# Head 1's output gates and values by seven half-size products, with the low parts of the sums of x on VectorE

## The chip, the cores and the metric

The kernel runs on one core of one Trainium2 chip. The metric is the device time of one execution in microseconds (us); the kernel before takes 1049.19 us (median of 3 runs, 1048.17 to 1050.72).

## The reference

One inference step of a two-layer decoder trunk. 1024 prompt tokens and 8 sequences of 4 new tokens, 1056 tokens in all, pass a gated linear recurrence (layer 0) and then HGRN2 attention with 8 heads of 128 channels (layer 1), each with a normalisation ahead, a projection in and a projection out. The change lies in layer 1:

```python
xn = _rmsnorm(x, g_norm)                        # (tokens, 1024)
u = (xn @ w_in).astype(jnp.float32)             # (tokens, 4 * 1024)
q, f, iv, gate = jnp.split(u, 4, axis=-1)       # per head: 128 columns of each
q = silu(q); log_g = ...f...; k = 1 - exp(log_g)
# chunked linear attention of every head over q, k, v = iv, decay log_g, state S
y = o * rsqrt(mean(o * o) + EPS) * o_gain * silu(gate)
return x + y @ w_out
```

A head has four projections, called items here: 0 queries, 1 forget gates, 2 values, 3 output gates. Each is a product of xn (1056 x 1024) with 1024 x 128 weights. All is float32.

## The kernel before, in words

**Products in three parts.** Every float32 operand is kept as a high part (hi) and a low part (lo) in the type fp32r, and a product is three matmuls (`mm3`, L253): L255 w_hi·x_hi, L256 w_hi·x_lo, L257 w_lo·x_hi. xn lies in SBUF as `xh` and `xl`, 8 tiles of 128 channels by 1056 tokens. A high part is a cast on ScalarE (ACT); a low part is a subtraction, `subtract` (L339), on GpSimd (POOL) or VectorE (DVE), whichever is passed to it as `e`.

**Direct items.** `product` (L405) makes one item for a third of the tokens (a chunk of 352): 8 tiles times 3 matmuls of 128 x 352. Heads 0 and 1 (`HC = 2`) are made so, one item and chunk after the other.

**Items by seven products.** From head 2 on, `seven(h, a, b, order, at)` makes two items a and b of a head together, by Strassen's scheme: seven products p1 to p7, each 512 channels by half the tokens, instead of eight. Each is made for two quarters of the tokens (x = 0, 1; 264 columns) in 4 x 3 matmuls, so a call has 7 x 2 x 12 = 168 matmuls of 128 x 264, and VectorE adds the products up (`plus`, L1521, 14 a call). The weights are combined by VectorE (`combine`, L1458, 4 of 512 columns a call), cast on ScalarE (L1448) and their low parts subtracted on GpSimd in halves of 256 columns (L339, `wlo`). `order` is a string such as "126b74b35": digits are products in order, "b" is the place of a *burst*, that is a piece of the attention of a head (`burst1` to `burst4`: its scores, its states and its outputs at several levels).

**Sums of x.** The products read x itself (p1, p2, p3) or sums of its quarters. Three of these sums, T2, T3 and T4 (tiles `t20` to `t41`; in lists of instructions `t_5227` and `t_5228` are T2 hi and lo, `t_5229` and `t_5230` T3, `t_5231` and `t_5232` T4), serve p6, p7 and p4. They are built once, in `build` and `parted_sum`, while heads 0 and 1 are projected: for each of 4 tiles and 2 quarters four loads of xn (264 columns each) into landing spots, three sums or differences by VectorE (L1389), three casts by ScalarE (L1392) and three low parts on GpSimd (L339): 24 of each in all. The landing spots are a ring of six pieces: two of the small tile `tmp` and four in `R[:, 3]`. The fourth one, T1, serves p5 and is written over the upper halves of `xh[0..3]` and `xl[0..3]` once nothing direct reads them any more (`build1`): 8 pieces, each with two loads, a difference (L1389), a cast (L1392) and a low part on VectorE (L339), through the two pieces of `tmp` as a ring.

**What sets the order.** The kernel isn't written out instruction by instruction: a list planner (`Flow`) is given every instruction with a priority and a modelled cost and writes one order for each engine; the engines then run their queues in order. `SPOTS` names after which direct chunk of head 1 the bursts stand. DMAs are issued by SyncE (SP) for the most part, and each waits there until its target is free.

**Around the change**, before: after head 0 stand head 1's items 0, 1, 3 and 2 by 12 direct products, with burst 1 and burst 2 of head 1 among the last six; then head 2 with its items 0 and 1 by `seven` in the order `FQ0 = "126b74b35"`. For head 1's item 1 ScalarE makes a tanh (L1031) and GpSimd two scalings (L1033 into `ST`, L1035 into `a`); from `ST` VectorE makes the decays in `R` by one operation over all tokens (L1087), and the scores of burst 1 (L1075) start from those.

Of the kernel before, what the change touches and what calls it, by code (L numbers as in the profile page):

```python
# [26 lines left out]
NMM = 3  # L27
HC = 2
NM7 = 3
FQ0, FQ, GV = "126b74b35", "12b675b43", "126b754b3"  # L30
CUT = 2
SPOTS, SPOTS0, SPOTS1 = (6, 9, 0, 2), (2, 5, -1, -1), (1, 5, 9, 13, 17, 20)
K2 = 8 - K1
RM, SM = 3, 6
OUT = ((0, 512), (512, 288), (800, 256))
# [5 lines left out]
TOK = SEQ + NB * NS  # L41
# [5 lines left out]
H = 8  # L47
EPS = 1e-6
HT, QT = TOK // 2, TOK // 4
# [174 lines left out]
def tile_trunk(ctx: ExitStack, tc: tile.TileContext, xT, prm, hc, w0, wg, wo0, w1, wo1, s_in,  # L224
               yT, h_out, c_out, sp_out, ss_out):
    nc = tc.nc
    V, S, G, T, Q = nc.vector, nc.scalar, nc.gpsimd, nc.tensor, nc.sync
# [11 lines left out]
    R = work.tile([128, 4, TOK], F32, tag="R", name="R")  # L239
# [10 lines left out]
    def chunk(c):  # L250
        return slice(c * CH, (c + 1) * CH)
# [59 lines left out]
    with ExitStack() as l0:  # L311
# [3 lines left out]
        def fixed(name, shape, dt=F32, pool=None):  # L315
            return (pool or pl).tile(shape, dt, tag=name, name=name)
# [10 lines left out]
        def act(n, emit, r, w, prio=5, more=0.0):  # L327
            fl.add("ACT", (0.09 + 0.00088 * n if fl.exact else 0.25 + 0.0007 * n) + more, emit, r, w, prio)
# [615 lines left out]
    with ExitStack() as l1:  # L944
# [6 lines left out]
        TB = {(n, i): fixed(f"t{n}{i}", [128, 4, HT], F32R, p1) for n in (2, 3, 4) for i in range(2)}  # L951
        tmp = fixed("tmp", [128, 2, QT], F32, p1)
# [19 lines left out]
        SG = [rows[1 + 2 * (h % 2)] for h in range(H)]  # L972
# [6 lines left out]
        SA = a_rows[1]  # L979
# [8 lines left out]
        def two(*name):  # L988
            return [(*name, i) for i in range(2)]
# [4 lines left out]
        def brow(h, i):  # L994
            return (Bs, eight("B")) if i else (B2, eight("B2"))
# [7 lines left out]
        def inherit(new, olds):  # L1003

            fl.readers.setdefault(new, []).extend(i for k in olds for i in (*fl.readers.get(k, ()), *([fl.writer[k]] if k in fl.writer else [])))
# [3 lines left out]
        def ykeys(m, a, n):  # L1009

            return [("Y", m, i) for i, (u, v) in enumerate(zip(CUTS, CUTS[1:])) if u < a + n and v > a]

        def thrice(o, x, r, key):

            act(96, lambda: S.copy(o.rearrange("p (j t) -> p j t", j=3), x[:, None, :].to_broadcast([128, 3, 32])), r, ((key,),), 2)

        def item(h, i):


            def evac(c, ps, pk):  # L1020
                q = chunk(c)
                ps = ps[:, :CH]
                if i == 2:
                    n = min(CH, SEQ - c * CH)
                    act(n, lambda: S.copy(VT[:, c * CH:c * CH + n], ps[:, :n]), (pk,), (("VT", c),), 0)
                    if n < CH:
                        thrice(vrep, ps[:, n:], (pk,), "vrep")
                    return
                if i == 1:
                    t, tk = next(ts)  # L1030
                    act(CH, lambda: S.activation(t, ps, AF.Tanh, scale=0.5), (pk,), (tk,), 0)  # L1031
                    g, (b, bk) = Gs, brow(h, 1)
                    pool(0.3 * CH, lambda: G.tensor_scalar(g[:, q], t, lc[:, h:h + 1], lbc[:, h:h + 1], op0=ALU.mult, op1=ALU.add),  # L1033
                         (tk,), GK, 0)
                    pool(0.3 * CH, lambda: G.tensor_scalar(b[:, q], t, lcn[:, h:h + 1], lc[:, h:h + 1], op0=ALU.mult, op1=ALU.add),  # L1035
                         (tk,), bk, 0)
                else:
                    o, k = (SG[h], ykeys(h % 2, c * CH, CH)) if i else arow(h, 0)
                    act(CH, lambda: S.activation(o[:, q], ps, AF.Silu), (pk,), k, 0)

            return w1[4 * h + i], evac
# [42 lines left out]
        def own_gate(h):  # L1084
            decay[h] = Gs, *GK
            (a, k0), (a1, k1) = arow(h, 0), arow(h, 1)
            dve(TOK, lambda: V.tensor_tensor(a1, a, Gs, op=ALU.mult), (*k0, *GK), k1, 1, True)  # L1087
# [258 lines left out]
        def burst1(h):  # L1346
            s = next(hg)
            run(together([*([levels01(h, *s)] if h < H else []), *([keys_(h - 1, *s), values(h - 1, *s)] if h else [])]))

        def burst2(h):  # L1350
            s = next(hg)
            run(together([*([levels24(h, *s)] if h < H else []), *([states(h - 1, *s), advance(h - 1, 0)] if h else [])]))

        def burst3(h):
            s = next(hg)
            run(together([*([outs(h - 1, *s), advance(h - 1, 1)] if h else []), *([levels816(h, *s)] if h < H else [])]))

        def burst4(h):
            s = next(hg)
            run(together([*([gated(h - 1, *s)] if h else []), *([levels3264(h, *s)] if h < H else [])]))  # L1360
            k = ()
            if h < H:
                turned(h, "vt", VT, [("VT", c) for c in range(4)], vflat, VK, vflat, VK)
                keys_turned(h)
                k = (("kt", "d", h % 2),)
            if 0 < h < H:
                dma(si.rearrange("p b v -> p (b v)"), s_in[h], k, two("si"), 4, 512)
            if 0 < h < H - 1:
                dma(yd[h - 1], SG[h - 1], (*ykeys((h - 1) % 2, 0, TOK), ("kt", 1)), (("yd", h - 1),), 4, 528)


        def build(j, temps):

            for x in range(2):
                lo, up = slice(x * QT, x * QT + QT), slice(HT + x * QT, HT + x * QT + QT)
                got = []
                for m, q in ((j + 4, up), (j, up), (j, lo), (j + 4, lo)):
                    t, tk = next(temps)
                    dma(t, xnd[m][:, q], (), (tk,), 5, 132)
                    got.append((t, tk))  # L1380
                (t, tk), (u, uk), (l, lk), (d, dk) = got
                add(QT, t, t, u, ALU.subtract, (tk, uk), tk)
                add(QT, l, l, t, ALU.add, (tk, lk), lk)
                add(QT, d, d, l, ALU.subtract, (dk, lk), dk)
                for n, o, k in ((3, t, tk), (2, l, lk), (4, d, dk)):
                    parted_sum(n, j, x, TB[n, 0][:, j, lo], TB[n, 1][:, j, lo], o, k, G)

        def add(n, o, a, b, op, r, w, prio=5):
            dve(n, lambda: V.tensor_tensor(o, a, b, op=op), r, (w,), prio, True)  # L1389
# [1 line left out]
        def parted_sum(n, j, x, hi, lo, t, tk, e, prio=5):  # L1391
            act(QT, lambda: S.copy(hi, t), (tk,), (("T", n, 0, j, x),), prio)  # L1392
            subtract(e, QT, lo, t, hi, (tk, ("T", n, 0, j, x)), (("T", n, 1, j, x),), prio)
# [143 lines left out]

        dma(si.rearrange("p b v -> p (b v)"), s_in[0], (), two("si"), 4, 512)
        own_gate(0)
        spots = [(R[:, 3, i * QT:i * QT + QT], ("tmp", 2 + i)) for i in range(4)]  # L1540
        small_ = [(tmp[:, i], ("tmp", i)) for i in range(2)]
        temps = cycle(small_ + spots)
        for j in range(4):
            build(j, temps)
        for h in range(HC):
            order = [item(h, i) for i in ((0, 1, 3, 2) if h else (3, 2))]
            seq_ = [(i, c) for i in range(len(order)) for c in range(NCH)]
            if h == HC - 1:
                seq_ = seq_[:-6] + [(len(order) - 2 + i, c) for c in (2, 1, 0) for i in (0, 1)]
            ws2 = {} if h else ahead  # L1550
            for n, (i, c) in enumerate(seq_):
                if i not in ws2:
                    ws2[i] = weights(order[i][0], 1024)
                order[i][1](c, *product(ws2[i], xcols(c)))
                if h and n == 5:
                    own_gate(h)
                for j, b in enumerate((burst1, burst2, burst3, burst4)):
                    if n == (SPOTS0, SPOTS)[h][j]:
                        b(h if j < 2 else h - 1)
# [3 lines left out]
        for i in range(6):  # L1563
            key = ("s", i)
# [3 lines left out]
        rawq = [next(raws) for _ in range(NRAW)]  # L1568
        for i in range(5 - NRAW):
            key = ("W", i)  # L1570
            inherit(key, [k for _, k in spots])
            rawq.append((R[:, 3, i * HT:i * HT + 512], key))


        for h in range(HC, H):
            seven(h, 0, 1, FQ0 if h == HC else FQ, (lambda h=h: burst3(h - 1), lambda h=h: burst4(h - 1)))
            own_gate(h)
            seven(h, 3, 2, GV, (lambda h=h: burst1(h), lambda h=h: burst2(h)))


        yh, yl = (list(o[:4]) for o in (xh, xl))
# [4 lines left out]
        for k in range(H):  # L1586
            if k < 4:
                olds = [("x", 1, k, x) for x in range(2)] + [("T", 1, i, k, x) for i in range(2) for x in range(2)]
            else:
                n, i = ((2, 0), (3, 0), (4, 0), (4, 1))[k - 4]  # L1590
# [22 lines left out]
        for i, o in enumerate(ks):  # L1613
            key = ("k", i, 1)
# [18 lines left out]
        for n, (m, c) in enumerate([(m, c) for c in range(NCH) for m in range(2)] + [(m, c) for m in range(2, KD) for c in range(NCH)]):  # L1633
# [9 lines left out]
            x, xk = x2[m][:, chunk(c)], ykeys(Y2 + m, c * CH, CH)  # L1643
# [13 lines left out]
        for m in range(KD):  # L1657
            row = (xh, xl)[m // 4][4 + m % 4]
            hi, lo, hk, lk = row[:, :nl], row[:, nl:2 * nl], ("late", m, 0), ("late", m, 1)
# [9 lines left out]
        for o, olds in ((R[:, 0], eight("A", 1)), (SA, [("SA", i) for i in range(2)]), (rows[5], VK),  # L1669
                        (SG[6], ykeys(0, 0, TOK))):  # L1670
            for a in (0, 512):
                key = ("spare", len(spare))
# [50 lines left out]
        for a, n in OUT:  # L1723
# [4 lines left out]
            for m in range(KD):  # L1728
# [5 lines left out]
                hi, lo, wk = late[m]  # L1734
# [7 lines left out]
                x, xk = x2[m][:, q], ykeys(Y2 + m, a, n)  # L1742
# [89 lines left out]
```

## Time and profile before

The profiled execution took 1049.25 us, of which its span (first to last instruction) is 1047.4 us.

| what | before |
|---|---|
| time, median of 3 runs | 1049.19 us |
| the profiled execution: time, span | 1049.25, 1047.4 us |
| busy: PE (matmul), DVE (VectorE) | 99%, 77% |
| busy: ACT (ScalarE), POOL (GpSimd) | 55%, 50% |
| chain that ended last: PE, DVE | 89%, 7% |
| TensorE from head 1's item 1 to the end of its direct products | 550.0 to 591.15 us |

In the page, engines are PE (TensorE's matmuls), PEld (its weight loads), DVE, ACT, POOL and SP; L339 is line 339 of the kernel. A row of a group gives `output<-inputs`, the shape, the count, the busy time and mean duration, and the idle time ahead of it with its releaser. Where the matmuls fill TensorE, an instruction of another engine costs time only if a matmul comes to wait for it.

### The profile page before, as it was taken

What the parts mean: (1) busy time and instruction counts of PE and PEld (TensorE: products, weight loads), DVE (VectorE), ACT (ScalarE), POOL (GpSimd) and SP (SyncE); (2) the same over time, 40 slices, a digit from 0 to 9 for tenths busy, and PEclk for the clock granted to TensorE, in tenths of its full rate; (3) what the DMA queues carried; (4) which work ended last, traced back from release to release, by engine and by line L of the source; (5) the groups of instructions that cost most, each with busy time, mean ns of one, the idle gap of its engine ahead of it and who ended that gap; (6) DMA issues with size and microseconds to landing.
All of it is one profiled execution on the core that took longest, in us unless ns stands there. A gap on an engine that the chain in (4) does not pass through costs nothing.

```text
span 1047.4 us, 25549 instructions
## 1 busy us (share of the span) xinstructions
PE 1036.1 (99%) x9836; PEld 1006.4 (96%) x9836; DVE 805.7 (77%) x1578; ACT 579.9 (55%) x1324; POOL 524.1 (50%) x601
## 2 busy tenths in 40 slices
PE   9999999999999999999999999999999999999997
PEld 9999999999999999999999999999999999999986
DVE  7999996788788599345586787897979797985436
ACT  6568656866775776334444364646454554652333
POOL 3425443544544255644756555555555555651544
PEclk9999999999999999999999999999999999999998
DMA  9201112123761586434554341423324242577204
GB/s 303 65 16 58 54 49 73 49 65 94 218 194 58 160 270 187 151 123 169 185 153 149 95 157 61 121 87 114 114 92 130 78 143 85 182 225 210 86 1 166
DMA packets 92009, 130.66 MB, mean 125 GB/s; under 512 B 11632, under 2 KB 70000, under 8 KB 91888
## 3 DMA queue, kind: packets, MB, share of 16 engines
q1 hardware_dynamic: 82672, 113.69, 34.9%
q10 hardware_dynamic: 9216, 15.35, 4.7%
q8 instruction: 77, 1.26, 0.5%
q14 instruction: 44, 0.36, 0.1%
HBM read 85.93 MB, written 38.20 MB: 119 GB/s over the span
## 4 chain that ended last, share of the span: by engine, by line
PE 89%; DVE 7%; DMA 1%; issue 1%; POOL 1%; ACT 0%; POOLq 0%; ACTq 0%; DVEq 0%
PE mm L255 25%; PE mm L257 25%; PE mm L256 25%; PE hg L1075 1%; PE hg L583 1%; PE hg L1289 1%; PE hg L255 1%; PE hg L1291 1%; PE hg L256 1%; PE hg L257 1%; PE hg L1237 1%; DMA wraw<-in_w_dram 1%; DVE R L449 1%; PE mm L1075 1%; PE hg L1266 1%
## 5 line engine op out<-in xcount | busy, mean ns | idle before, releaser
L255 PE MATMUL mm<-xh,whi 128*128 128x352 f32 (+1 forms) x1143 | 358.9, 314 | 0.6 <-DVE k L1521 0.6
L257 PE MATMUL mm<-xh,wlo 128*128 128x352 f32 (+1 forms) x1143 | 353.3, 309 | 0.0
L256 PE MATMUL mm<-xl,whi 128*128 128x352 f32 (+1 forms) x1143 | 353.0, 309 | 0.0
L339 POOL TENSOR_TENSOR wlo<-wraw,whi 128x256 fp32r<-128x256 f32 (+3 forms) x184 | 200.3, 1104 | 197.9 <-ACT whi L394 94.8
L255 PEld LDWEIGHTS mm<-xh,whi 128*128 128x128 f32 x1143 | 214.7, 188 | 2.9 <-DVE k L1521 1.0
L256 PEld LDWEIGHTS mm<-xl,whi 128*128 128x128 f32 x1143 | 214.9, 188 | 1.5
L257 PEld LDWEIGHTS mm<-xh,wlo 128*128 128x128 f32 x1143 | 214.8, 188 | 0.3 <-POOL wlo L339 0.3
L515 DVE SCALAR_TENSOR_TENSOR k<-xb,prm_sb,k 128x352 f32<-128x352 f32 (+2 forms) x144 | 90.0, 637 | 10.9 <-ACT k L512 7.7
L255 PE MATMUL mm<-t,whi 128*128 128x264 f32 (+1 forms) x306 | 89.4, 292 | 0.0
L257 PE MATMUL mm<-t,wlo 128*128 128x264 f32 (+1 forms) x306 | 87.6, 286 | 0.0
L256 PE MATMUL mm<-t,whi 128*128 128x264 f32 (+1 forms) x306 | 87.5, 286 | 0.0
L339 POOL TENSOR_TENSOR wlo<-R,whi 128x256 fp32r<-128x256 f32 x64 | 59.0, 941 | 32.9 <-ACT whi L1448 14.7
L1521 DVE TENSOR_TENSOR k<-mm,k 128x264 f32<-128x264 f32 x144 | 59.9, 423 | 19.0 <-PE mm L257 18.3
L598 POOL TENSOR_TENSOR k<-X 128x352 f32<-128x352 f32 x36 | 45.8, 1282 | 48.4 <-DVE R L599 39.2
L394 ACT CAST whi<-wraw 128x512 fp32r<-128x512 f32 (+2 forms) x83 | 46.3, 574 | 37.4 <-PE mm L256 18.7
L255 PEld LDWEIGHTS mm<-t,whi 128*128 128x128 f32 x306 | 57.5, 188 | 0.5
L256 PEld LDWEIGHTS mm<-t,whi 128*128 128x128 f32 x306 | 57.6, 188 | 0.0
L257 PEld LDWEIGHTS mm<-t,wlo 128*128 128x128 f32 x306 | 57.6, 188 | 0.0
L1448 ACT CAST whi<-wraw 128x512 fp32r<-128x512 f32 x52 | 32.0, 617 | 33.6 <-PE mm L256 14.1
L255 PE MATMUL mm<-yh,whi 128*128 128x352 f32 x153 | 49.9, 326 | 0.0
L257 PE MATMUL mm<-yh,wlo 128*128 128x352 f32 x153 | 49.4, 323 | 0.0
L256 PE MATMUL mm<-yl,whi 128*128 128x352 f32 x153 | 49.4, 323 | 0.0
(457 smaller groups left out, 2537.6 us busy)
## 6 DMA issues: line engine op xcount, KB each, us to landing
wraw<-in_w_dram SPq DMA_DIRECT2D x57, 256.0 KB, 3.1
wraw<-in_w_dram ACTq DMA_DIRECT2D x35, 256.0 KB, 3.2
wraw<-in_wo_dram SPq DMA_DIRECT2D x34, 192.0 KB, 2.6
si<-in_s_in_dram SPq DMA_DIRECT2D x8, 512.0 KB, 5.8
vt<-sg SPq DMA_DIRECT2D x8, 512.0 KB, 3.2
sg<-vt SPq DMA_DIRECT2D x32, 128.0 KB, 2.9
kt<-kt SPq DMA_DIRECT2D x8, 512.0 KB, 2.6
sg<-kt SPq DMA_DIRECT2D x32, 128.0 KB, 3.4
```

The lines of the kernel that those rows point to most:

```text
L255: T.matmul(out, wh, xh, start=first, stop=False)
L256: T.matmul(out, wh, xl, start=False, stop=False)
L257: T.matmul(out, wl, xh, start=False, stop=last)
L339: emit = lambda: e.tensor_tensor(b, x, a.bitcast(F32), op=ALU.subtract)
L394: act(m, lambda hi=hi, raw=raw, m=m: S.copy(hi[:, :m], raw[:, :m]), rk, (hk,), prio)
L449: (pool if e is G else dve)(CH, lambda: e.tensor_tensor(a[:, :CH], a[:, :CH], sq, op=ALU.add), (sk, ak), (ak,), 2)
L515: dve(u, lambda src=src, dst=dst, sh=sh, k=k: V.scalar_tensor_tensor(dst, sh(src, k), pc("cw", 12 * k + m), dst, op0=ALU.mult, op1=ALU.add ...
L583: fl.add("PE", 0.62, lambda ps=ps, i=i, c=c: T.matmul(ps[:96, :CH], gs[:, i, :], ST[:96, chunk(c)], start=True, stop=True), (("gs",), *((" ...
L598: pool(CH, lambda x=x, a=a, b=b: G.tensor_tensor(x, a.bitcast(F32), b.bitcast(F32), op=ALU.add), (ak, bk), (xk,), 3)
L1075: T.matmul(ps[32 * j:32 * j + 32, n * w:n * w + w], B[:, o:o + 32], q(slice(o, o + 32)), start=True, stop=True, tile_position=(0, 32 * j))
L1448: act(512, lambda: S.copy(hi, raw), (rk,), (hk,), 2)
L1521: dve(QT, lambda: V.tensor_tensor(o[0], z[0], u[0], op=ALU.add), (z[1], u[1]), (o[1],), 0)
```

## The change

- Head 1 makes only its items 0 and 1 by direct products; its items 3 and 2 go through `seven(1, 3, 2, GV0)`, with `GV0 = "126b74b35"`, and bursts 1 and 2 of head 1 stand at the two "b" of it. Item 1's chunks run from the last to the first. Head 2's first call loses its own order and takes that of the later heads (`FQ = "12b675b43"`).
- The 24 low parts of T2, T3 and T4 are subtracted by VectorE (`V`), no longer by GpSimd (`G`).
- The pieces of xn for T2 to T4 land in eight spots in rows that are used later (`SG[1]`, head 1's output gates, in lists of instructions `sg`, and `SA`, in lists `a`), no longer in two of `tmp` and four of `R[:, 3]`; `R[:, 3]`, which holds raw weights in `seven`, no longer has to wait for them. The pieces are built first for quarter 0 of all four tiles, then for quarter 1.

```diff
-FQ0, FQ, GV = "126b74b35", "12b675b43", "126b754b3"
+FQ, GV0, GV = "12b675b43", "126b74b35", "126b754b3"
...
-SPOTS, SPOTS0, SPOTS1 = (6, 9, 0, 2), (2, 5, -1, -1), (1, 5, 9, 13, 17, 20)
+SPOTS, SPOTS0, SPOTS1 = (-1, -1, 0, 2), (2, 5, -1, -1), (1, 5, 9, 13, 17, 20)
...
-        def build(j, temps):
+        def build(x, temps):
 
-            for x in range(2):
+            for j in range(4):
...
                 for n, o, k in ((3, t, tk), (2, l, lk), (4, d, dk)):
-                    parted_sum(n, j, x, TB[n, 0][:, j, lo], TB[n, 1][:, j, lo], o, k, G)
+                    parted_sum(n, j, x, TB[n, 0][:, j, lo], TB[n, 1][:, j, lo], o, k, V)
...
-        spots = [(R[:, 3, i * QT:i * QT + QT], ("tmp", 2 + i)) for i in range(4)]
+        spots = [(o[:, i * QT:i * QT + QT], ("spot", n, i)) for n, o in enumerate((SG[1], SA)) for i in range(4)]
         small_ = [(tmp[:, i], ("tmp", i)) for i in range(2)]
-        temps = cycle(small_ + spots)
-        for j in range(4):
-            build(j, temps)
+        temps = cycle(spots)
+        for x in range(2):
+            build(x, temps)
+        for n, keys in enumerate((ykeys(1, 0, TOK), two("SA"))):
+            for k in keys:
+                inherit(k, [k for _, k in spots[4 * n:4 * n + 4]])
         for h in range(HC):
-            order = [item(h, i) for i in ((0, 1, 3, 2) if h else (3, 2))]
+            order = [item(h, i) for i in ((0, 1) if h else (3, 2))]
             seq_ = [(i, c) for i in range(len(order)) for c in range(NCH)]
             if h == HC - 1:
-                seq_ = seq_[:-6] + [(len(order) - 2 + i, c) for c in (2, 1, 0) for i in (0, 1)]
+                seq_ = seq_[:-6] + [(len(order) - 2 + i, c) for i in (0, 1) for c in (2, 1, 0)]
...
             key = ("W", i)
-            inherit(key, [k for _, k in spots])
             rawq.append((R[:, 3, i * HT:i * HT + 512], key))
 
-        for h in range(HC, H):
-            seven(h, 0, 1, FQ0 if h == HC else FQ, (lambda h=h: burst3(h - 1), lambda h=h: burst4(h - 1)))
-            own_gate(h)
-            seven(h, 3, 2, GV, (lambda h=h: burst1(h), lambda h=h: burst2(h)))
+        for h in range(HC - 1, H):
+            if h >= HC:
+                seven(h, 0, 1, FQ, (lambda h=h: burst3(h - 1), lambda h=h: burst4(h - 1)))
+                own_gate(h)
+            seven(h, 3, 2, GV if h >= HC else GV0, (lambda h=h: burst1(h), lambda h=h: burst2(h)))
```

**GpSimd's queue where head 1's forget gates are scaled.** The row order before, from the first chunk's pair (L1033, L1035) to the last (the rows between stand in front of the decays of L1087):

```order
L1033 TENSOR_SCALAR ST<-k,smalls 128x352
L1035 TENSOR_SCALAR a<-k,smalls 128x352
L339 TENSOR_TENSOR t_5230<-tmp,t_5229 128x264
L339 TENSOR_TENSOR t_5228<-R,t_5227 128x264
L339 TENSOR_TENSOR t_5232<-R,t_5231 128x264
L339 TENSOR_TENSOR t_5230<-R,t_5229 128x264
L1033 TENSOR_SCALAR ST<-k,smalls 128x352
L1035 TENSOR_SCALAR a<-k,smalls 128x352
L339 TENSOR_TENSOR t_5228<-tmp,t_5227 128x264
L339 TENSOR_TENSOR t_5232<-tmp,t_5231 128x264
L339 TENSOR_TENSOR wlo<-wraw,whi 128x512
L1033 TENSOR_SCALAR ST<-k,smalls 128x352
```

The same place in the order of the change (`wlo` are low parts of weights, the last of 512 columns for a direct item and those of 256 for head 1's call of `seven`):

```order
L339 TENSOR_TENSOR wlo<-wraw,whi 128x512 x2
L339 TENSOR_TENSOR wlo<-R,whi 128x256 x2
L339 TENSOR_TENSOR wlo<-wraw,whi 128x256 x2
L1033 TENSOR_SCALAR ST<-k,smalls 128x352
L1035 TENSOR_SCALAR a<-k,smalls 128x352 x2
L1033 TENSOR_SCALAR ST<-k,smalls 128x352 x2
L1035 TENSOR_SCALAR a<-k,smalls 128x352
L339 TENSOR_TENSOR wlo<-wraw,whi 128x256 x4
```

Six low parts of sums and one of weights between the first and the last scaling are gone; the three pairs stand directly behind each other, and two products' weights stand ahead of them, four pieces behind.

**VectorE's queue where the last pieces of T1 are made** (`xl<-tmp,xh` is the low part of a piece, `tmp<-xl,tmp` the difference ahead of it). Before, beside the first call of `seven`, which is head 2's:

```order
L1458 TENSOR_TENSOR wraw<-R,wraw 128x512
L1458 TENSOR_TENSOR R<-R,wraw 128x512
L1389 TENSOR_TENSOR tmp<-xl,tmp 128x264 x2
L339 TENSOR_TENSOR xl<-tmp,xh 128x264 x2
L1521 TENSOR_TENSOR k<-mm,k 128x264 x3
L1389 TENSOR_TENSOR tmp<-xl,tmp 128x264
L1521 TENSOR_TENSOR k<-mm,k 128x264
L339 TENSOR_TENSOR xl<-tmp,xh 128x264
```

And in the change, beside head 1's call (`k<-mm,k` and `sg<-mm,k` add products up; L1079 masks scores of burst 2):

```order
L1521 TENSOR_TENSOR sg<-mm,k 128x264 x2
L1458 TENSOR_TENSOR R<-wraw 128x512
L1389 TENSOR_TENSOR tmp<-xl,tmp 128x264 x2
L339 TENSOR_TENSOR xl<-tmp,xh 128x264
L1521 TENSOR_TENSOR k<-mm,k 128x264
L339 TENSOR_TENSOR xl<-tmp,xh 128x264
L1458 TENSOR_TENSOR wraw<-wraw 128x512
L1521 TENSOR_TENSOR k<-mm,k 128x264
L1079 COPY_PREDICATED attnd<-mask_90,hg 128x256
L1079 COPY_PREDICATED attnd<-mask_91,hg 128x256
```

The last two pieces now stand between additions of head 1's call itself, whose products they hold up if they are late, and a combination of head 2's weights stands in front of them.

## The prediction

> **What bounds the kernel now.** I read the page first: busy times, the granted clock (PEclk), the chain that ended last, then TensorE's groups.
>
> ```profile
> span 1047.4 us, 25549 instructions
> PE 1036.1 (99%) x9836; PEld 1006.4 (96%) x9836; DVE 805.7 (77%) x1578; ACT 579.9 (55%) x1324; POOL 524.1 (50%) x601
> PEclk9999999999999999999999999999999999999998
> PE 89%; DVE 7%; DMA 1%; issue 1%; POOL 1%; ACT 0%; POOLq 0%; ACTq 0%; DVEq 0%
> L257 PEld LDWEIGHTS mm<-xh,wlo 128*128 128x128 f32 x1143 | 214.8, 188 | 0.3 <-POOL wlo L339 0.3
> ```
>
> TensorE is busy 99% at full clock, and an operand that this kernel prepares is hardly ever late: 0.3 us over 1143 weight loads. So time changes by what TensorE has to do, and by new waits of TensorE. The profiled execution took 1049.25 us, its span 1047.4, so 1.85 lies outside; I sum against 1049.25, which is 0.06 above the median 1049.19, less than the runs differ.
>
> **Part 1: fewer matmul columns.** The granted clock is 1.00 in all three of these windows of L256's matmuls, one third of a product's matmuls: one window of direct products (16 x 3 = 48 matmuls of 352 columns), two of a call of seven (72 and 120 of 264).
>
> ```profile
> core 0: us, PE busy (x) PEld busy (x), PEclk, DMA share, GB/s
> 583.50:591.15 7.65, 5.12 (x16) 3.01 (x16) 1.00 0.17 46
> 643.43:652.21 8.78, 6.79 (x24) 4.51 (x24) 1.00 0.22 69
> 668.97:683.70 14.73, 11.33 (x40) 7.52 (x40) 1.00 0.61 176
> ```
>
> 7.65 / 48 = 159.4 ns for 352 columns; (8.78 + 14.73) / 192 = 122.4 ns for 264. Head 1's items 3 and 2 are 2 items x 3 chunks x 24 = 144 matmuls now, 144 x 159.4 ns = 22.95 us; afterwards 7 x 2 x 12 = 168, 168 x 122.4 ns = 20.56 us. **-2.4 us.** The columns alone would give 12.5% off; the rows give 10.4%, since a matmul costs some 11 ns beside its columns in both. The bursts have the same matmuls before and after, and head 2 has the same products in another order: 0.
> The Trainium skill ("TensorE: Matmul & The Clock Gate", section "Back-to-back issue gap") puts a stream of weight loads and matmuls at about 81 ns for 128 columns and 131 ns for 512, the narrow one being dearer per column. Read straight between these, as an estimate, that is 110 and 99 ns, and 168 narrow matmuls would cost 0.7 us more than 144 wide ones: the sum would be 1049.8 us. This trace disagrees with its 159.4 and 122.4 ns, and the measurement decides; the rule gets no chance of its own.
>
> **Part 2: low parts off GpSimd.** The chain of waits shows where GpSimd ends last before burst 1, TensorE's waits what it cost, and the tile rows the 24 low parts.
>
> ```profile
> 557.95 0.47 ACT k L1031
> ...
> 558.79 0.76 POOL t L339
> 559.54 0.80 POOL ST L1033
> ...
> 561.13 0.65 POOL t L339
> 561.81 0.45 POOL t L339
> ...
> 562.54 1.29 POOL wlo L339
> 563.83 0.63 POOL ST L1033
> 564.48 1.27 DVE R L1087
> 565.80 1.10 PE hg L1075 x64
> ...
> PE hg L1075 <- DVE R L1087: 0.2, 1, 0.2
> ...
> L339 POOL TENSOR_TENSOR t<-R,t x15: 751/762/1225, 515.1 to 558.8; 128x264 fp32r<-128x264 f32 x15
> L339 POOL TENSOR_TENSOR t<-tmp,t x9: 755/759/1232, 505.4 to 561.8; 128x264 fp32r<-128x264 f32 x9
> ```
>
> Between the tanh at 557.95 and the decays at 564.48 stand low parts of sums (0.76 + 0.65 + 0.45) and of weights (1.29). They leave this chain, and burst 1 moves from 565.8 to about 570 (behind p1, p2 and p6), so its wait goes: 0.2 us, and about as much where the chain passes on to the next product; I take **-0.4** (bounds 0 and -0.6). What is late next is the weights of p6 and p7, four pieces behind the scalings; GpSimd has its 24 x 0.76 = 18 us of low parts less by then, so I count 0.
> VectorE now makes the 24. Its own idle time, where it waits for DMA in these 90 us, and its load by stage:
>
> ```profile
> DVE R L1389 <- DMA R<-xn: 8.5, 4, 6.8
> DVE tmp L1389 <- DMA tmp<-xn: 7.8, 3, 3.6
> ...
> 550.00:591.20 41.20, 40.95 (x454) 39.67 (x451) 28.60 (x61) 16.84 (x43) 21.80 (x26) 1.00 0.41 122
> 656.70:683.80 27.10, 27.10 (x380) 26.58 (x379) 24.05 (x51) 15.78 (x38) 13.82 (x15) 1.00 0.46 138
> ...
> L1521 DVE TENSOR_TENSOR k<-mm,k x144: 394/422/435, 596.4 to 923.3; 128x264 f32<-128x264 f32 x144
> L1458 DVE TENSOR_TENSOR wraw<-wraw x19: 674/679/3075, 573.0 to 896.6; 128x512 f32<-128x512 f32 x19
> ...
> L339 DVE TENSOR_TENSOR xl<-tmp,xh x8: 423/692/969, 576.4 to 601.0; 128x264 fp32r<-128x264 f32 x8
> ```
>
> (The two windows give us, then busy time and count of PE, PEld, DVE, ACT, POOL.) A low part on VectorE is 0.42 us at best; 24 are 10 us against 16 us of waiting for DMA, and eight spots in place of six let loads start earlier. **0** up to 550 us.
>
> **Part 3: VectorE in head 1's stage.** It is busy 28.60 of 41.2 us now. Added are 14 additions of 0.42 (5.9), 4 combinations of 0.68 (2.7) and about 6 low parts (3.3 at 0.55, half way between 0.42 and 0.69). The updates of the state now stand behind p5:
>
> ```profile
> L1057 DVE TENSOR_TENSOR R<-R,sg 128x512 f32<-128x512 f32 (+1 forms) x4 | 2.8, 689 | 0.0
> L1257 DVE SCALAR_TENSOR_TENSOR a<-a,gp,hg 128x128 f32<-128x128 f32 x7 | 2.4, 345 | 0.1
> L1273 DVE SCALAR_TENSOR_TENSOR si<-si,gp,hg 128x128 f32<-128x128 f32 x4 | 1.1, 339 | 0.0
> ```
>
> 2.4 + 1.1 and three of 0.69, 5.6 us. That makes 34.9 of 38.3 us, 91%, as much as the steady half call 656.70 to 683.80, where 24.05 of 27.10 (89%) left TensorE without a wait. So it fits, with little to spare. I take **+0.3** for short waits; bounds 0 and, below as rival 1, 4.6.
>
> **Part 4: T1 in time for p5.** T1's chain of pieces runs through two spots, from the first load to the last low part:
>
> ```profile
> 567.95 2.75 SPq L325 DMA_DIRECT2D xl<-xn  x4
> ...
> 588.93 7.93 SPq L325 DMA_DIRECT2D tmp<-xn  x3
> ...
> 592.87 1.86 DVE L1389 TENSOR_TENSOR tmp<-xl,tmp 128x264 f32<-128x264 f32 x2
> 594.65 1.86 DVE L339 TENSOR_TENSOR xl<-tmp,xh 128x264 fp32r<-128x264 f32 x2
> ...
> 601.00 0.83 DVE L339 TENSOR_TENSOR xl<-tmp,xh 128x264 fp32r<-128x264 f32 x1 [0.21 <-ACT xh L1392]
> ...
> 592.40 5.40 POOL L339 TENSOR_TENSOR wlo<-wraw,whi 128x256 fp32r<-128x256 f32 x6 [0.18 <-ACT whi L1448]
> ...
> 565.80:567.40 1.60, 1.60 (x71) 1.51 (x71) 1.29 (x2) 0.25 (x1) 1.60 (x2) 1.00 0.05 18
> 579.30:583.50 4.20, 4.20 (x164) 3.80 (x164) 2.92 (x9) 1.76 (x5) 0.10 (x1) 1.00 0.40 112
> ```
>
> (The last two rows are windows of TensorE's at bursts 1 and 2.) The chain took 601.83 - 567.95 = 33.9 us, but much of that was waiting, since its loads stood in SP's queue behind the last chunks (3 in 7.93 us) and it had time until p5 of head 2. Afterwards item 1's chunks run from the last to the first, so its first load may start when the last chunk's product ends, at 553.9 (550.0 and 24 x 159.4 ns = 3.8), and the last piece is needed at 586.2: item 1 ends at 550.0 + 11.5 = 561.5; p1, p2, p6 (2.94 each), burst 1 (1.6), p7, p4, burst 2 (4.2) and p3 take 23.4, to 585.0; p5 reads tile 3 about 1.2 later. Allowed: 32.3 us for 16 operations on VectorE, 8 casts and 16 loads of 2 to 4 us, three deep. I take 0 (bounds 0 and 6.2).
>
> **Part 5: later heads.** TensorE waits for additions 0.6 us in all behind 592 us.
>
> ```profile
> PE mm L255 <- DVE k L1521: 0.6, 2, 0.4
> ```
>
> Head 2's new order may save or add some: 0 (bounds -0.6 and +1).
>
> **Sum:** -2.4 - 0.4 + 0.3 = -2.5; 1049.25 - 2.5 = 1046.7 us.
>
> **Rivals.** *1. VectorE late, held up by GpSimd.* At 592.87 and 594.65 a pair of VectorE's subtractions from SBUF took 0.93 us each instead of 0.42 while GpSimd ran six low parts of weights. If the 16 operations of T1 and the combinations meet GpSimd so, 16 x 0.5 = 8 us come on top: 42.9 for 38.3, up to 4.6 us late, 1051.0 us. Half of the meetings would make 0.6 by the sum, but VectorE's work comes in bouts, and I take the middle, 2.3: 1049.25 - 2.8 + 2.3 = 1048.8 (1047.0 to 1051.0), and the gain is eaten. For it: GpSimd has six low parts of weights a product pair here, too. Against: the median L1458 is 0.679, undisturbed.
> The Trainium skill ("SBUF — State Buffer", section "SBUF: two separate sides") has a rule for it: a VectorE operation with two SBUF inputs and a GpSimd operation share one pair of ports, which the one that starts first locks for its whole length while the other fully blocks. The trace agrees (0.93 against 0.42); by that rule without gaps in GpSimd's row the full 4.6 us would come, by the median row none.
> *2. Slower: p5 waits for T1.* Mechanism: the two-spot ring in `build1`, whose last piece p5 needs at 586.2. It decides from a chain of over 32.3 us. With the 33.9 measured before p5 waits 1.6 us (1048.3); the kernel is slower by more than 0.2%, 2.1 us, when the chain reaches 32.3 + 2.5 + 2.1 = 36.9; with rival 1's full 4.6 on the 33.9 it is 38.5, a wait of 6.2 and 1052.9. For it: the same ring, VectorE fuller. Against: its waits before were on spots and loads in SP's queue, which the last direct chunks no longer share.
> *3. More gain:* head 2's first call has T1 ready and its weights split ahead, the 0.6 us go, no new waits come: 1045.8 (1045.4 to 1046.1).
> *4. It does not do what it says:* the head's products stay as they are: 1049.2. The order speaks against it.
>
> **How the numbers follow.** About 0.2% (2.1 us) is what a measurement of this kernel tells from no change: faster means below 1047.1, slower above 1051.3. Forecast, 1046.2 to 1047.6: 0.52 (faster 0.40, same 0.12, since short waits of 0.7 us in place of 0.3 reach the bound). Rival 1: 0.26 (faster 0.03, same 0.22, slower 0.01). Rival 2: 0.10 (same 0.02, slower 0.08). Rival 3: 0.10, faster. Rival 4: 0.02, same. Faster 0.53, same 0.38, slower 0.09. The range is 1045.4 to 1049.2: it takes in rival 3, the forecast and most of rival 1, and leaves out rival 2's slower part and rival 1's worst, about 0.13 together, and some hundredths below 1045.4.
>
> **What would show it.** TensorE: 168 matmuls of 264 columns for head 1 at 122 ns, head 2's first product starting near 588.3, 2.8 us earlier. No wait on L1087. GpSimd: pairs L1033, L1035 back to back. Rival 1: waits of `mm` on `L1521` between 561 and 592 and L1389 or L339 at 0.9 us. Rival 2: a wait at p5 on the low part `xl` (L339) or its load near 586. The prediction is wrong if these waits exceed 1 us in sum, or if TensorE's work there falls by other than 2.4.

## The result, and the profile after

The changed kernel takes **1047.07 us** (median of 18 runs, 1046.26 to 1048.02), the kernel before 1048.98 us in the same comparison: a ratio of 0.9984, 95% interval 0.9977 to 0.999, so 1.05 to 2.4 us less. The profiled execution took 1046.93 us. A second set of 11 runs of the changed kernel gave 1047.73 against 1048.93 and the same ratio of 0.9984 (0.9975 to 0.9993). The ratio on record is not the quotient of the two medians, which would be 0.9989 here.

The page of after, its first lines and the chain that ended last:

```profile
span 1045.1 us, 25638 instructions
PE 1033.6 (99%) x9860; PEld 1004.5 (96%) x9860; DVE 824.2 (79%) x1620; ACT 582.9 (56%) x1327; POOL 511.3 (49%) x587
...
PE 88%; DVE 8%; DMA 2%; issue 1%; POOL 0%; ACTq 0%; ACT 0%; POOLq 0%; SPq 0%; DVEq 0%
```

TensorE has 24 matmuls more and 2.5 us less work, and VectorE is busy 18.5 us longer. VectorE's share of the chain that ended last reads 8% here and 7% before, but it is 7% again in a second profile of the change, so nothing is read from it.

The table cuts the span at places that both programs have (the first product matmul behind a burst 4), and shows in which stage the 2.3 us of the two spans lie. Times of before and after, from the two traces:

| stage on TensorE | before | after | difference |
|---|---|---|---|
| start to head 1's item 1 | 550.00 | 549.29 | -0.71 |
| head 1's item 1 to the end of its burst 4 (in head 2's first call) | 63.77 | 60.90 | **-2.87** |
| from there to the end of head 6's burst 4 (in head 7's first call) | 276.82 | 276.93 | +0.11 |
| the last stage, to the end of head 7's burst 4 (among the output products) | 54.88 | 57.28 | **+2.40** |
| from there to the end | 101.95 | 100.73 | -1.22 |

The windows of the second and the fourth stage, first of before and then of after (us, then busy time and count of PE, PEld, DVE, ACT, POOL), and last the part of the second that the prediction summed for VectorE:

```profile
550.00:613.75 63.75, 63.50 (x793) 61.11 (x789) 45.19 (x91) 29.46 (x84) 38.12 (x43) 1.00 0.38 117
890.60:945.45 54.85, 54.85 (x762) 52.96 (x759) 48.37 (x104) 32.81 (x91) 30.61 (x34) 1.00 0.62 194
...
549.30:610.20 60.90, 60.90 (x817) 58.83 (x814) 56.66 (x111) 29.86 (x82) 39.77 (x47) 1.00 0.33 101
887.10:944.40 57.30, 55.39 (x763) 53.08 (x759) 49.07 (x104) 33.08 (x91) 30.98 (x34) 1.00 0.60 186
...
549.30:587.60 38.30, 38.30 (x477) 37.34 (x475) 35.16 (x66) 16.42 (x41) 25.58 (x30) 1.00 0.44 131
```

In the first row of after TensorE is busy for all of the 60.90 us, in the second it is idle for 1.9 of 57.30. In the last stage VectorE and GpSimd have as many operations as before (104 and 34). The waits of TensorE behind 590 us say on what:

```profile
PE mm L255 <- DVE k L1521: 2.4, 4, 1.1
```

Before it was 0.6 us, and none of it behind 890. GpSimd's scalings stand as the order had it, without low parts of sums between them, and T1's last piece (`xl<-tmp,xh`) comes at 584.63:

```profile
557.80 1.21 POOL L1035 TENSOR_SCALAR a<-k,smalls 128x352 f32<-128x352 f32 x1 [2.08 <-ACT k L1031]
558.99 1.33 POOL L1033 TENSOR_SCALAR ST<-k,smalls 128x352 f32<-128x352 f32 x1
561.62 0.64 POOL L1033 TENSOR_SCALAR ST<-k,smalls 128x352 f32<-128x352 f32 x1 [1.30 <-ACT k L1031]
562.23 1.16 POOL L1035 TENSOR_SCALAR a<-k,smalls 128x352 f32<-128x352 f32 x1
...
584.63 0.42 DVE L339 TENSOR_TENSOR xl<-tmp,xh 128x264 fp32r<-128x264 f32 x1
```

**What took the last stage's 2.4 us.** VectorE's timeline of after near 908, and GpSimd's beside it:

```profile
907.86 0.43 DVE L1521 TENSOR_TENSOR k<-mm,k 128x264 f32<-128x264 f32 x1
908.21 2.90 DVE L1057 TENSOR_TENSOR sg<-a,sg 128x528 f32<-128x528 f32 x1
911.03 0.42 DVE L1521 TENSOR_TENSOR sg<-mm,k 128x264 f32<-128x264 f32 x1
...
907.17 1.70 POOL L1216 TENSOR_TENSOR vb<-vst,bm 96x256 fp32r<-96x256 f32 x2 [1.31 <-DVE vst L1203]
908.83 1.71 POOL L339 TENSOR_TENSOR t<-wraw,t 128x128 fp32r<-128x128 f32 x2
```

The same operation of before, at the same place of the program:

```profile
911.67 0.70 DVE L1057 TENSOR_TENSOR sg<-a,sg 128x528 f32<-128x528 f32 x1
...
910.62 2.21 POOL L1216 TENSOR_TENSOR vb<-vst,bm 96x256 fp32r<-96x256 f32 x2 [1.31 <-DVE vst L1203]
912.80 1.71 POOL L339 TENSOR_TENSOR t<-wraw,t 128x128 fp32r<-128x128 f32 x2
```

The operation takes 0.70 us before and 2.90 after, with the same four operations of GpSimd beside it and the same ones directly ahead of it. In both traces it starts some 0.05 us ahead of GpSimd's second `vb`. Before, VectorE got in, and that `vb` took 1.12 us. After, the `vb` got in (0.61 us), the two low parts followed without a gap until 908.83 + 1.71 = 910.54, and VectorE's operation ended only behind them, at 911.11. The two additions queued behind it came at 911.03 and 911.38, and TensorE waited 0.8 us for them.

About ten us later two more additions stand in VectorE's row behind updates of the state, and TensorE waits 1.1 us again, until 921.9. The other 0.5 us of the stage's 2.4 are in TensorE's busy time (55.39 against 54.85) and are not traced further.

What decides who gets in is not shown. Five traces of kernels with head 1's call have the hold of 2.90 us (the change, the same a second time, and three of its variants: lows_back, p5_early, old_spots); those of the kernel before and two of its variants (lows_only, before_act_dma) have the 0.70. VectorE's lead over the second `vb` is 51 to 56 ns in the five and 50 to 54 in the three, so the lead doesn't tell. In the five the first wait is 0.8 us each time, the second between 0.4 and 1.5, so the second is not the hold's alone.

### The profile page after: what moved, and what is told of

Its sections match the earlier page's. It is cut to its first block, busy times and chain, and to the rows that moved or that the text cites. A ratio compares the mean times of both kernels' runs of the same rounds, so it can differ in the third digit from the quotient of the medians.

```text
span 1045.1 us, 25638 instructions
## 1 busy us (share of the span) xinstructions
PE 1033.6 (99%) x9860; PEld 1004.5 (96%) x9860; DVE 824.2 (79%) x1620; ACT 582.9 (56%) x1327; POOL 511.3 (49%) x587
## 4 chain that ended last, share of the span: by engine, by line
PE 88%; DVE 8%; DMA 2%; issue 1%; POOL 0%; ACTq 0%; ACT 0%; POOLq 0%; SPq 0%; DVEq 0%
PE mm L255 25%; PE mm L257 24%; PE mm L256 24%; PE hg L1075 2%; PE hg L583 1%; PE hg L1289 1%; DMA wraw<-in_w_dram 1%; PE hg L255 1%; PE hg L1291 1%; PE hg L256 1%; PE hg L257 1%; DVE a L1257 1%; DVE sg L1057 1%; DVE R L1057 1%; PE hg L1333 1%
## 5 line engine op out<-in xcount | busy, mean ns | idle before, releaser
L255 PE MATMUL mm<-xh,whi 128*128 128x352 f32 (+1 forms) x1127 | 352.5, 313 | 0.7 <-DVE k L1521 0.5
L257 PE MATMUL mm<-xh,wlo 128*128 128x352 f32 (+1 forms) x1127 | 346.9, 308 | 0.0
L256 PE MATMUL mm<-xl,whi 128*128 128x352 f32 (+1 forms) x1127 | 346.7, 308 | 0.0
L339 POOL TENSOR_TENSOR wlo<-wraw,whi 128x256 fp32r<-128x256 f32 (+3 forms) x188 | 203.9, 1100 | 207.1 <-ACT whi L394 103.0
L255 PE MATMUL mm<-t,whi 128*128 128x264 f32 (+1 forms) x330 | 96.5, 292 | 0.8 <-DVE k L1521 0.8
L257 PE MATMUL mm<-t,wlo 128*128 128x264 f32 (+1 forms) x330 | 94.5, 286 | 0.0
L256 PE MATMUL mm<-t,whi 128*128 128x264 f32 (+1 forms) x330 | 94.3, 286 | 0.0
L339 POOL TENSOR_TENSOR wlo<-R,whi 128x256 fp32r<-128x256 f32 x70 | 63.7, 931 | 47.6 <-ACT whi L1448 30.7
L1521 DVE TENSOR_TENSOR k<-mm,k 128x264 f32<-128x264 f32 x154 | 64.2, 423 | 16.5 <-PE mm L257 15.8
L255 PEld LDWEIGHTS mm<-t,whi 128*128 128x128 f32 x330 | 62.0, 188 | 1.6 <-DVE k L1521 1.0
L257 PEld LDWEIGHTS mm<-t,wlo 128*128 128x128 f32 x330 | 62.1, 188 | 0.2 <-POOL wlo L339 0.2
L256 PEld LDWEIGHTS mm<-t,whi 128*128 128x128 f32 x330 | 62.1, 188 | 0.0
```

What stands on the lines that cost most here:

```text
L255: T.matmul(out, wh, xh, start=first, stop=False)
L256: T.matmul(out, wh, xl, start=False, stop=False)
L257: T.matmul(out, wl, xh, start=False, stop=last)
L339: emit = lambda: e.tensor_tensor(b, x, a.bitcast(F32), op=ALU.subtract)
L1521: dve(QT, lambda: V.tensor_tensor(o[0], z[0], u[0], op=ALU.add), (z[1], u[1]), (o[1],), 0)
```

## The experiments

Each was timed beside the kernel before, in three later sessions on the chip (before 1049.12, 1048.93 and 1048.88 us); the first two rows are those of the first comparison. "Head 1" and "last" are the second and fourth stage of the table above, in us, each from one profiled execution. The reversed chunks of item 1 and the new order of building the sums were not undone by themselves.

| kernel | median us | ratio to before, 95% interval | head 1 | last |
|---|---|---|---|---|
| before | 1048.98 | 1 | 63.77 | 54.88 |
| the change | 1047.07 | 0.9984 (0.9977 to 0.999) | 60.90 | 57.28 |
| lows_only | 1049.87 | 1.001 (1.0001 to 1.0019) | 63.80 | 54.93 |
| lows_back | 1048.8 | 0.9997 (0.9988 to 1.0006) | 62.38 | 57.11 |
| fq0_back | 1047.01 | 0.9982 (0.9973 to 0.9991) | 60.97 | 55.85 |
| p5_early | 1047.85 | 0.999 (0.9981 to 0.9999) | 60.73 | 57.62 |
| after_again | 1047.73 | 0.9984 (0.9975 to 0.9993) | 61.06 | 57.15 |
| wt_v | 1046.06 | 0.9968 (0.9957 to 0.998) | 60.90 | 55.16 |
| old_spots | 1047.62 | 0.999 (0.9981 to 0.9999) | 60.78 | 56.52 |
| wt_v_fq0 | 1045.85 | 0.9972 (0.9961 to 0.9982) | 61.05 | 54.99 |
| before_act_dma | 1049.41 | 1.0004 (0.9995 to 1.0013) | 63.71 | 54.90 |
| wt_v_before | 1049.21 | 1.0002 (0.9993 to 1.0011) | 63.79 | 54.92 |

**Theory**: the change saves what head 1's stage has less of matmul work and waits, and loses most of it again in the last stage (head 7), where a VectorE operation is held by GpSimd. **Rivals**: the loss is head 2's new order; the low parts alone are the gain; T1 was nearly late.

### lows_only: the low parts alone

```diff
 (the kernel before)
-                    parted_sum(n, j, x, TB[n, 0][:, j, lo], TB[n, 1][:, j, lo], o, k, G)
+                    parted_sum(n, j, x, TB[n, 0][:, j, lo], TB[n, 1][:, j, lo], o, k, V)
```

> The kernel before with one edit: the 24 low parts of T2, T3 and T4 are subtracted by VectorE instead of GpSimd. Theory: the low parts leave GpSimd's chain ahead of burst 1, so the wait of burst 1 on the decays (L1087, 0.2 us) and the gap of about 0.25 us at the next product's low weights go: -0.4 us, 1048.6 against 1048.98, a ratio of 0.9996 that its interval can hardly part from 1; VectorE gains 10 us of work by 565 us and no wait of TensorE on it appears. Rival A (VectorE too full): new waits on L1389 or L339 or on additions in head 2, slower by 1 us or more. Rival B: the two gaps were not GpSimd's, and they stay.

The -0.4 did not come: head 1's stage is 63.80 us, as before. The rows of this kernel around burst 1's decays, and TensorE's wait there:

```profile
564.02 3.56 POOL L339 TENSOR_TENSOR wlo<-wraw,whi 128x512 fp32r<-128x512 f32 x2
...
564.09 2.34 DVE L1087 TENSOR_TENSOR R<-R,ST 128x1056 f32<-128x1056 f32 x1 [1.43 <-POOL ST L1033]
...
PE hg L1075 <- DVE R L1087: 0.5, 1, 0.5
```

The low parts of weights, which stood ahead of the last scaling, now start beside the decays and hold those for 1.1 us (2.34 against 1.27): what was taken out of the chain came back as a hold on its next link. Ahead of 549 us a further wait of 0.7 us appears (L1129 on L1057). The low parts alone lose, by about 0.1%.

### lows_back: the change without its low parts on VectorE

```diff
-                    parted_sum(n, j, x, TB[n, 0][:, j, lo], TB[n, 1][:, j, lo], o, k, V)
+                    parted_sum(n, j, x, TB[n, 0][:, j, lo], TB[n, 1][:, j, lo], o, k, G)
```

> The change with one part undone: the 24 low parts are back on GpSimd. Theory: GpSimd again has them between the scalings of the forget gates and the low parts of head 1's weights, so p6 and p7 wait for low weights (0.1 us in the change) and burst 1 for its decays; 0.5 to 2 us slower than the change, 1047.6 to 1049. Rival A: GpSimd had room (it is idle 11.5 us ahead of 549 in the change), no difference from the change within 0.3 us. Rival B: VectorE, freed of 10 us, loses the waits in the later heads, faster than the change.

The size was right (62.38 against 60.90 in head 1's stage), the place wasn't: neither p6 nor burst 1 waits. VectorE and GpSimd of this kernel, and the wait:

```profile
577.15 3.47 DVE L339 TENSOR_TENSOR xl<-tmp,xh 128x264 fp32r<-128x264 f32 x1
...
576.90 1.37 POOL L1216 TENSOR_TENSOR vb<-vst,bm 96x256 fp32r<-96x256 f32 x2
578.24 1.41 POOL L339 TENSOR_TENSOR wlo<-wraw,whi 128x256 fp32r<-128x256 f32 x2
579.61 1.59 POOL L339 TENSOR_TENSOR wlo<-R,whi 128x256 fp32r<-128x256 f32 x2
...
PE mm L1237 <- DVE kst L1203: 1.3, 1, 1.3
```

With 24 operations more, GpSimd's row has no gap from 571 to 581; a low part of T1 that takes 0.42 us alone takes 3.47, and burst 2 waits for the operation queued behind it. So the low parts on VectorE are worth 1.5 us to head 1's call, though nothing to the kernel before. VectorE, with 24 operations less, was held all the same in the last stage (57.11 us), so rival B falls.

### fq0_back: head 2 in its old order

```diff
-                seven(h, 0, 1, FQ, (lambda h=h: burst3(h - 1), lambda h=h: burst4(h - 1)))
+                seven(h, 0, 1, "126b74b35" if h == HC else FQ, (lambda h=h: burst3(h - 1), lambda h=h: burst4(h - 1)))
```

> The change with one part undone: head 2's first call has its own order 126b74b35 again. Theory: head 1's stage stays 2.8 us shorter; the waits of TensorE behind 592 us (2.4 us in the change, 1.9 of them at 910 and 921 in head 7) come from where single VectorE operations meet GpSimd's, which any edit ahead of them moves, so they change but not in a sense that follows from head 2: 0.3 to 3 us, 1045 to 1047.8. Rival: head 2's order is their cause, and they fall to the 0.6 us of before, 1045.2 us.

Its time is the change's, 1047.01. Waits of TensorE for additions are 1.2 us by the trace, neither the 0.6 of the rival nor 2.4: in its last stage another operation of the same chain (L1057, `R<-R,sg`, at 907.11) is held 2.48 us, and less waits behind it (last stage 55.85). That stage is 1.4 us shorter than the change's, but the median shows no gain. In this one trace the start up to layer 0's gates (the first L583) is 0.9 us longer and the end 0.8; whether that goes for the other runs is not known. Head 2's order is not the cause by itself: with the old one another operation meets GpSimd.

### p5_early: is T1 a near miss?

```diff
-FQ, GV0, GV = "12b675b43", "126b74b35", "126b754b3"
+FQ, GV0, GV = "12b675b43", "126b74b53", "126b754b3"
```

> The change with p5 ahead of p3 in head 1's call (126b74b53). Theory: in the change the last piece of T1 is done at 585.05 and first read at about 585.75; p5 one product earlier would read it at 582.8, so TensorE waits about 2.2 us there for a low part of T1 (xl), and the time is 2.2 us above the change, 1049.3. Rival: the planner draws T1's pieces ahead of other work of VectorE because they are due earlier, and the wait stays below 1 us, 1047 to 1048; the margin of 0.7 us was then no near miss.

The theory fell and the rival held. Head 1's stage has no wait (60.73), since the last piece came three us earlier, in time for a need at 582.8:

```profile
581.51 0.42 DVE L339 TENSOR_TENSOR xl<-tmp,xh 128x264 fp32r<-128x264 f32 x1
```

The planner moved T1's pieces ahead in VectorE's queue when they were due earlier, so the margin of 0.7 us in the change tells of that order and not of a limit. The 0.8 us over the change's median came behind: 0.76 in the next stage (55.79 against 55.03) and 0.3 in the last.

### after_again: what comes back

No edit.

> The change once more, nothing edited, for what of its profile comes back. Theory: everything between head 1's first item and the last head's outputs is set by the orders of the queues and comes back within 0.1 us: the stage from head 1's item 1 to the end of head 2's first burst 4 takes 60.9 us, the last stage 57.3, with one VectorE operation held about 2.9 us near 908; the start (69.25 us to the first L583) and the end behind the last matmul scatter by 0.5 to 1 us. Rival: the meeting with GpSimd near 908 goes by nanoseconds, is absent this time, and the last stage takes 55 to 56.

Head 1's stage and the last came back to 0.16 and 0.13 us, the operation near 908 again as `sg<-a,sg` of 2.90 us (at 909.10), with waits of 1.8 us behind it. So the hold comes back in the same program, and the rival falls. The span of this execution was 1.3 us longer than that of the first: 0.38 ahead of head 1's item, 0.16 in head 1's stage, 0.35 between, -0.13 in the last stage, and 0.51 behind it, where the last two matmuls took 1.22 us in place of 0.70.

### wt_v: take GpSimd's run away

```diff
-                ws2[m] = weights(wo1[m][:, :128 * K1], 128 * K1, at=at_)
+                ws2[m] = weights(wo1[m][:, :128 * K1], 128 * K1, 2, V if at_ else G, at_)
```

> The change with one edit: the low parts of the first two output weights (four subtractions, t<-wraw,t) are made by VectorE and no longer by GpSimd. Theory: GpSimd's unbroken run from 907 to 910.5 is gone, the L1057 operation at 908 takes 0.7 us instead of 2.9, TensorE's waits of 1.0 and 1.1 us in the last stage fall to some 0.3 together, and the last stage takes 55.3 to 56.0 instead of 57.3: 1045.5 to 1046.0 us. Rival: the 2 us of new work on VectorE make the additions as late as the hold did; last stage 57 and more, no gain.

As the theory had it: 55.16 us in the last stage, and 1046.06 in all, 1.0 us under the change's first median and 1.7 under that of the same session. The intervals of the two ratios overlap a little, but only one of its six runs took longer than the fastest of the change's 29 (1046.15). The chain's last operation and the stage:

```profile
908.21 0.69 DVE L1057 TENSOR_TENSOR sg<-a,sg 128x528 f32<-128x528 f32 x1
...
887.95:943.10 55.15, 55.09 (x762) 53.01 (x760) 48.60 (x108) 33.24 (x91) 24.29 (x30) 1.00 0.62 193
...
910.23 1.18 POOL L1216 TENSOR_TENSOR vb<-vst,bm 96x256 fp32r<-96x256 f32 x2 [5.03 <-DVE vst L1203]
```

2.90 us has become 0.69, and TensorE's idle time in the stage 0.06 where it was 1.9; the second wait is gone too. The edit also let the planner put `vst` behind that chain, so that GpSimd's `vb` start two us later; which of the two freed it isn't told apart.

### wt_v_before: the same edit on the kernel before

The same two lines, in the kernel before.

> The kernel before with one edit: the low parts of the first two output weights are made by VectorE, the edit that took 2.1 us from the last stage of the change. Theory: before has no such hold in its last stage (54.88 us, longest VectorE operation there 1.79 with no wait of TensorE behind it), so the edit brings nothing, 1048.7 to 1049.3, last stage 54.8 to 55.3; the 2.4 us that it can bring in the change were then lost by the change. Rival: the edit is a gain of its own in any order, 1047 to 1047.5.

1049.21 us, last stage 54.92: nothing.

```profile
889.40:944.30 54.90, 54.89 (x761) 52.94 (x759) 50.95 (x108) 32.81 (x91) 24.33 (x30) 1.00 0.62 194
```

So the edit is no gain of its own, and the 2.1 us that it brings back in the last stage are of the 2.4 that the change lost there.

### old_spots: the landing spots

```diff
-        spots = [(o[:, i * QT:i * QT + QT], ("spot", n, i)) for n, o in enumerate((SG[1], SA)) for i in range(4)]
+        spots = [(R[:, 3, i * QT:i * QT + QT], ("tmp", 2 + i)) for i in range(4)]
...
-        temps = cycle(spots)
+        temps = cycle(small_ + spots)
...
-        for n, keys in enumerate((ykeys(1, 0, TOK), two("SA"))):
-            for k in keys:
-                inherit(k, [k for _, k in spots[4 * n:4 * n + 4]])
...
             key = ("W", i)
+            inherit(key, [k for _, k in spots])
```

> The change with one part undone: the pieces of xn land in two pieces of tmp and four of R[:,3] again. Theory: fewer spots, and the raw weights of head 1's call that lie in R[:,3] wait for the last piece; GpSimd's low parts of those weights come later (they stand behind the first scalings in the order), and a hold of VectorE or a wait for low weights appears between 561 and 592: 0.3 to 1.5 us slower than the change in the stage of head 1 (61.2 to 62.4 instead of 60.9). Rival: the spots make no difference, 60.9 again.

The rival held: head 1's stage takes 60.78 us, and the whole 1047.62, against 1047.73 of the change in the same session. In its trace the stretch from the start of layer 0's gates (L583) to head 1's item takes 480.81 us where the change has 480.05, with a wait of 0.4 (L1129 on ScalarE's copy), so the new spots may save something there. Its last stage is 0.76 us shorter than the change's, and the median shows neither.

### wt_v_fq0: both edits together

The edits of wt_v and fq0_back.

> The change with both edits: the four low parts of output weights on VectorE, and head 2's first call in its old order 126b74b35. Theory: stage of head 1 61.0, last stage 55.3 to 55.8, waits for additions below 1 us in all: 1045 to 1046 us, faster than the change by 1 to 2 us. Rival: as for the first edit alone, the added work on VectorE eats it, 1047.

1045.85 us, 0.9972 of before: the lowest median of all, though not to be told from wt_v. Waits for additions are down to 0.6 us, as before the change.

### before_act_dma: the end

In the table of stages the end is 1.22 us shorter, with the same matmuls. ScalarE's last copy and its last output DMA, in before and then in after:

```profile
1040.44 0.37 ACT L1713 COPY sg<-hg 128x256 f32<-128x256 f32 x1 [1.97 <-PE hg L1700]
1043.44 1.02 ACTq L325 DMA_DIRECT2D out_yT_dram<-sg  x1
```

```profile
1038.86 0.37 ACT L1716 COPY sg<-hg 128x256 f32<-128x256 f32 x1 [1.45 <-PE hg L1703]
1041.59 0.40 ACTq L325 DMA_DIRECT2D out_yT_dram<-sg  x1
```

From the copy to the end it is 6.98 us before and 6.27 after. (The other 0.5 us: the last two matmuls ahead of the copy took 1.22 us in before and 0.70 in after; in after_again 1.22 too, so that is scatter.)

```diff
 (the kernel before)
-                    ws2[i] = weights(order[i][0], 1024)
+                    ws2[i] = weights(order[i][0], 1024, 2, G, None, S if h and i > 1 else Q)
```

> The kernel before with one edit: the four raw-weight loads of head 1's items 3 and 2 are issued by ScalarE, as head 1's call of seven does, and no longer by SyncE; ScalarE then issues 68 DMAs and SyncE 643, as in the change, instead of 64 and 647. From ScalarE's last copy to the end, before and the low-parts-only kernel took 6.98 and 6.96 us, the change and five of its variants 6.25 to 6.28. Theory: that 0.7 us hangs on which DMAs stand on which queue, not on anything on TensorE, and this kernel ends 6.25 to 6.3 us after that copy, 0.7 us of the change's gain by itself: 1048.3. Rival: it comes with the change's products, and the end stays at 6.97.

```profile
1040.37 0.37 ACT L1713 COPY sg<-hg 128x256 f32<-128x256 f32 x1 [1.45 <-PE hg L1700]
1043.10 0.40 ACTq L325 DMA_DIRECT2D out_yT_dram<-sg  x1
```

The end became 6.25 us, with not one matmul changed: the 0.7 us come with four loads moved from one queue to the other. (wt_v_before, with the loads on SyncE as before, ends in 6.79 us, so the gain is 0.5 to 0.7.) The whole kernel gained nothing (1049.41). Its trace shows 1.3 us more from layer 0's gates to head 1's item, 0.9 of it in two waits of TensorE (0.6 for a low part of xn, 0.3 at L1129); whether the edit brings these was not tried.

## Why the prediction held, and where it did not

- **Fewer columns, -2.4: right.** The products of head 1's call take 121.9 ns each in after (48 in the row below), as the rows of before said, and 168 of them are there.

```profile
581.73:587.58 5.85, 4.53 (x16) 3.02 (x17) 1.00 0.06 19
```

- **Waits around burst 1, -0.4: right in sum, wrong in its reason.** Together with the columns, head 1's stage is 2.87 us shorter (2.71 in the second profile), where -2.8 was summed. But the wait did not go because low parts left GpSimd's chain (lows_only: 0.5 us in place of 0.2); it went because burst 1 moved behind three products. In lows_back, with the low parts on GpSimd and burst 1 moved, it doesn't wait either.
- **Short waits in head 1's stage, +0.3: there were none.** VectorE's load came out as summed (35.16 us of 38.30 against 34.9), but by errors that cancel, and these are the largest two. The four combinations were counted as 2.7 us of new work, though the window of before has three already (2.88 us, and 2.72 after). T1's sixteen operations were not counted as new work, though the window of before holds only ten of them, 4.8 us, and that of after all sixteen, 12.0 us. Sixteen of 0.42 would be 6.7 us, so some 5 us come on top, all in operations that stand beside GpSimd at work. So rival 1's hold came here, two thirds of its 8 us, and TensorE did not wait for it. T1's rows of after (ns, shortest, median and longest):

```profile
L1389 DVE TENSOR_TENSOR tmp<-xl,tmp x8: 386/658/964, 556.3 to 583.2; 128x264 f32<-128x264 f32 x8
L339 DVE TENSOR_TENSOR xl<-tmp,xh x8: 418/827/1495, 558.2 to 584.6; 128x264 fp32r<-128x264 f32 x8
```

- **T1 in time for p5, 0: right.** Its chain took from 552.35 to 585.05, 32.7 us against 32.3 allowed, with some 0.7 us to spare at p5.
- **Later heads, 0 (bounds -0.6 and +1): this is the step that failed.** It cost 2.3 to 2.4 us in the last stage, of which wt_v brings 2.1 back, where wt_v_before has nothing to bring back. The prediction looked for VectorE held by GpSimd in head 1's stage, where VectorE gets more work, and put rival 1 there. The hold that TensorE waited for came six heads later, where neither engine has more operations than before. The edit shifts the planner's order there too, but the operations at the meeting stand in the same order in both traces, so why the change loses the meeting stays open.
- **The end, not in the sum: -0.7**, from the queues on which four loads stand.

The parts that come back from one profile to the next are -2.8 (head 1), +2.3 (last stage), -0.7 (the end) and +0.1 or +0.45 between, some -0.9 us; the timed runs say -1.05 to -2.4. The remainder isn't found: starts and ends scatter by 0.5 to 1 us from one execution to the next, and the traces show one or two of these each. That the predicted 1046.7 lies 0.4 us off the first median, and 1.0 off the second, is thus partly luck: an unseen loss and an unseen gain.

## What to carry to other kernels

Where a planner or scheduler makes the order, an edit in one stage can change the order in those that follow; compare stage by stage down to the end, and look for single operations that take several times their median. Here the gain stood in the edit's own stage and the loss elsewhere, and a second small edit won it back (1 to 1.7 us more). Moving operations from one engine to a fuller one paid only together with the step that needed the first engine's queue (1.5 us in head 1's call, nothing alone).

## What the hardware showed

- A VectorE operation with two SBUF operands that meets GpSimd can be held through several of its instructions, not one: 2.90 us in place of 0.70 through three (after), 3.47 in place of 0.42 through five (lows_back). It is not held to the end of a run in every case: in lows_back it was done at 580.62, while GpSimd's unbroken run lasted until 581.20, and in before the same operation got in behind the first `vb`, and GpSimd's second one took longer instead (1.12 us in place of 0.61). The Trainium skill ("SBUF — State Buffer", section "SBUF: two separate sides") says that whichever starts first holds the shared ports for the whole instruction while the other fully blocks. These rows agree with the block; who started first doesn't tell before from after, since VectorE's record starts 0.05 us ahead of the second `vb` in both.
- Four loads on ScalarE's queue in place of SyncE's (68 and 643 DMAs in all, where 64 and 647 stood) shortened the end, hundreds of us later, from 6.79 to 6.98 us in three traces to 6.25 to 6.28 in nine (last copy of ScalarE to the end). Why is left open.
